# Hybrid decoder trunk on one core: SwiGLUs 2 to 4 with one plain block and five pairs, reciprocal-root factors, and block 0's second weight parts by accumulating DMA

## The chip, the cores and the metric

The kernel runs on one core of a Trainium2 chip. The metric is the device time of one execution in microseconds (us). The kernel before takes 1728.46 us, the median of 3 runs (1728.2 to 1728.85).

## What is computed

Two layers over 512 tokens of width 1024, all in float32. Each layer is

```python
x = x + 0.5 * swiglu(rms_norm(x, ffn1_norm[l]), ffn1_wg[l], ffn1_wu[l], ffn1_wd[l])
h = rms_norm(x, mix_norm[l])
z = h @ w_in[l]            # attention heads and a gated short convolution
x = x + concat([attn_out, conv_out]) @ w_out[l]
x = x + 0.5 * swiglu(rms_norm(x, ffn2_norm[l]), ffn2_wg[l], ffn2_wu[l], ffn2_wd[l])
```

with `swiglu(h, wg, wu, wd) = (silu(h @ wg) * (h @ wu)) @ wd`, 2816 columns in `wg` and `wu`, and a last `rms_norm`. So there are four SwiGLUs: number 1 opens layer 0, number 2 ends it, numbers 3 and 4 do the same in layer 1.

## The kernel before

**Three matmuls for one.** Every float32 operand is split into a rounded first part (`hi`) and the remainder (`lo`), and a product is `hi*hi + hi*lo + lo*hi`. `split` (L185) makes the two parts of a weight unit: ScalarE (ACT in the profile) casts `hi` (L186), VectorE (DVE) subtracts to get `lo` (L187). A weight unit is 512 KB in SBUF, 128 partitions by 1024 numbers. `need_split` (L189) makes the parts of unit n+2 when the group of unit n is taken (`SPLIT_AHEAD = 2`). The parts rotate through three buffers each (`wh`, `wl`), so the parts of unit n+3 can be made once the matmuls of unit n are through. Raw weights come from HBM through SyncE's queue into eight buffers tagged `raw`, four units ahead or more (`need_raw`, L173). Where a form needs the sum of two weights, GpSimd (POOL) issues a second, accumulating DMA into the same raw buffer (L181).

**Blocks.** The 2816 columns are 11 blocks of 256. A *plain* block (`plain`, L587) is 4 groups of 24 matmuls of 512 columns (`group`, L233): two gate groups and two up groups. Its gate is `silu(acc * inv) * inv`, because the groups run on the unnormalised `x * gain` while the norm's factors `inv` are still being made. A *Winograd* block (`winograd`, L608) works on the normalised input: seven half products (`CHAINS`, L46) of 24 matmuls of 256 columns. A *pair* (`winograd2`, L682) does two blocks at once with seven half products of 24 matmuls of 512 columns; each of its seven steps takes two weight units, h = 0 and 1. A pair's result lies token by token, so it is turned afterwards by 16 transposes in 4 turns (`turn`, L740), which wait in a list `pending` and are issued one by one by `flush`.

**Forms.** The seven half products need seven forms of the normalised input, `b11, b21, t2, t3, t1, t4, b22` in this order. `scale` (L407) makes the normalised input `full` (tile `hf`) with 8 DVE instructions, and `make` (L424) builds a form from it: sums on DVE where the form has them, then a split.

**Order of a SwiGLU.** `STAGES` writes it out: plain blocks 0 and 1, the down projection of block 0 (`("d", (0,))`, 8 groups of 6 matmuls), pair 2, down of block 1, pair 4, down of 2 and 3, pair 6, down of 4 and 5, pair 8, down of 6 and 7, Winograd block 10, down of 8, 9, 10. The forms are made during plain block 1 and the down projection of block 0, with `t4` and `b22` right after it. Inside this order the framework's scheduler places the instructions of each engine when the kernel is built: on an engine, the first in program order that it expects to be ready goes next.

**Norm.** While the stage before ends, `take` (L354) and `square` (L365) prepare each chunk of `x` as it is finished. `factors` (L391) sums the squares over partitions with two matmuls (tile `ssq`), placed inside the second group at its step 5. Then come ACT's square root (tile `root`, L404), ACT's mean (L405), and on DVE a reciprocal (L342) and one Newton step (L343 to L345), which give `inv`.

**End.** In the last SwiGLU `Finale` transposes `x` during block 10 and computes the down projection of blocks 8, 9, 10 token by token, in two halves of 512 columns, with the last norm's root after each group of tokens (`root`, L843).

Of the kernel before, what the change touches and what calls it, by code (L numbers as in the profile page):

```python
# [51 lines left out]
def trunk_kernel(  # L52
# [136 lines left out]
    def need_split(g):  # L189
        while state["split"] <= min(g, len(order) - 1):  # L190
            n = state["split"]
            u, what = order[n]
            if what is None or what == "wide":
# [78 lines left out]
    def plan():  # L272
        def cols(src, k0, kc, n):
            wide = abreast(kc)
            for b in range(0, n, wide):
                order.append((add_unit((src, k0, kc, b * P, wide * P)), None))

        def up(wg, wu, b):
            if b < PLAIN:
                for w in (wg, wu):  # L280
                    for j in range(2):
                        order.append((add_unit((w, 0, KC, (2 * b + j) * P, P)), None))
                return
# [21 lines left out]
        def ffn(wg, wu, wd, last=False):  # L305
            for what, b in STAGES:
# [6 lines left out]
                if not last or b[-1] < FF // (2 * P) - 1:  # L313
                    cols(wd, 2 * b[0], 2 * len(b), KC)
                    continue
# [6 lines left out]
        for l in range(DEPTH):  # L322
            ffn(ffn1_wg[l], ffn1_wu[l], ffn1_wd[l])
# [4 lines left out]
            ffn(ffn2_wg[l], ffn2_wu[l], ffn2_wd[l], l == DEPTH - 1)  # L328
# [11 lines left out]
    def newton(out, root, mean, spare):  # L340

        nc.vector.reciprocal(spare, root)  # L342
        nc.vector.tensor_mul(out, spare, spare)  # L343
        nc.vector.scalar_tensor_tensor(mean, mean, -0.5, out, op0=ALU.mult, op1=ALU.mult)
        nc.vector.scalar_tensor_tensor(out, mean, 1.5, spare, op0=ALU.add, op1=ALU.mult)  # L345

    class Norm:
# [32 lines left out]
        def groups(self, n, accs=()):  # L380
# [3 lines left out]
            while len(accs) < n:  # L384
                at, step = (1, 5) if self.i else (3, 2)
# [6 lines left out]
        def factors(self, parts):  # L392
# [11 lines left out]
            nc.scalar.activation(r, sp, AF.Sqrt, scale=1.0 / D, bias=eps)  # L404
            nc.scalar.activation(v, sp, AF.Identity, scale=1.0 / D, bias=eps)  # L405
            newton(self.inv, r, v, r)

        def scale(self):
# [12 lines left out]
            self.sums = [stock(f"sum{n}_{self.i}", shape=(P, KC // 2, H)) for n in range(2)]  # L421
# [107 lines left out]
    with tc.manual_schedule(engines={pe, act, dve}):  # L529
# [4 lines left out]
        first = group(norm.h, arrive)  # L534
# [6 lines left out]
    def first_parts():  # L541
# [3 lines left out]
        nc.scalar.activation(r, v, AF.Sqrt, scale=1.0 / D, bias=eps)  # L545
        nc.vector.tensor_scalar(v, v, 1.0 / D, EPS, op0=ALU.mult, op1=ALU.add)
        newton(y, r, v, r)
# [35 lines left out]
    def ffn(norm, after=None, late=None):  # L583

        acts = {}

        def plain(b):  # L587
# [16 lines left out]
            if norm.inv is None:  # L604
                accs = norm.groups(4, [first] if norm.i == 0 else [])
# [18 lines left out]
        def winograd(b, between=None):  # L624
# [18 lines left out]
            for step, (acc, operand, start) in enumerate(CHAINS):  # L643
# [34 lines left out]
                if between:  # L678
                    between(step)
            acts[b] = (hi, lo)  # L680

        def winograd2(b):  # L682
# [3 lines left out]
            accs = {  # L686
                c: [psum(tag, [P, S], f"{c}_{name}_{u}") for u in range(2)]
                for c, tag in (("x", "mm"), ("y", "sc"), ("w", "aux"))
            }
# [8 lines left out]
            for step, (acc, operand, start) in enumerate(CHAINS):  # L698
                xh, xl = norm.forms[operand]
                for h in range(2):  # L700
# [36 lines left out]
                    flush()  # L737
# [16 lines left out]
        def flush():  # L754
            if pending:
                pending.pop(0)()

        end = None
        for i, (what, b) in enumerate(STAGES):
            if what == "w":  # L760
                winograd2(b)
            if what == "u" and b < PLAIN:
# [3 lines left out]
            elif what == "u":  # L766
                if after is None:
                    end = Finale()
                winograd(b, end and end.step)
            if what != "d":  # L770
                continue
            rhs = [(acts[k][0][:, j, :], acts[k][1][:, j, :]) for k in b for j in range(2)]
            final = i + 1 == len(STAGES)
            if final and end:
                end.down(rhs)
# [10 lines left out]
            if b == (0,):  # L786
# [4 lines left out]
    class Finale:  # L791
# [3 lines left out]
        def __init__(self):  # L795
            self.y = [
                g4(f"ytok{t}", F32, (P, D)) if t < 2 else stock(f"ytok{t}", shape=(P, D))
                for t in range(NT)
            ]
# [3 lines left out]
        def step(self, n):  # L803

            for at in (0, 1) if n == 0 else (n + 1,):
                t, half = divmod(at, 2)
                tp = psum("mm", [P, S], f"yt_{t}_{half}")
# [8 lines left out]
        def widen(self, half, pairs):  # L816
            for i in range(pairs):
                if half == 0:
                    _, hi, lo = take_split()
                else:  # L820
                    u = len(units) - pairs + i
                    need_raw(u)
                    hi, lo = (form(f"ww{n}_{i}", shape=(P, 2, S)) for n in "hl")
                    split(hi, lo, raw_of.pop(u))
                self.w[half].extend((hi[:, k, :], lo[:, k, :]) for k in range(2))

        def piece(self, rhs, half, t, c0, wide, ssq):

            tok = slice(t * P, (t + 1) * P)
            acc = psum("mm", [P, wide], f"end_{half}_{t}_{c0}")  # L830
            cols = slice(c0, c0 + wide)
            for k, (ah, al) in enumerate(rhs):
# [3 lines left out]
                nc.tensor.matmul(acc, al[:, tok], wh[:, cols], start=False, stop=k == len(rhs) - 1)  # L836
# [4 lines left out]
            if half == 0:  # L841
                nc.gpsimd.tensor_mul(y, y, self.gain[half][:, cols])

        def root(self, t, ssq, rest):

            r, v, y = (small(f"{n}_end{t}", 1) for n in "rvy")
            nc.scalar.activation(r, ssq, AF.Sqrt, scale=1.0 / D, bias=rest)
            nc.vector.scalar_tensor_tensor(v, ssq, 1.0 / D, rest, op0=ALU.mult, op1=ALU.add)
            nc.vector.reciprocal(y, r)
            nc.vector.tensor_mul(r, y, y)  # L850
            nc.vector.scalar_tensor_tensor(r, r, -0.5, v, op0=ALU.mult, op1=ALU.mult)
            nc.vector.scalar_tensor_tensor(y, r, 1.5, y, op0=ALU.add, op1=ALU.mult)
            return y

        def down(self, rhs):
# [7 lines left out]
            self.widen(0, len(rhs) // 2)  # L863
            for t in range(NT):
                rest = done[:, t : t + 1]
                self.piece(rhs, 0, t, 0, S, rest)
                nc.vector.tensor_scalar(rest, rest, 1.0 / D, EPS, op0=ALU.mult, op1=ALU.add)
                if t == 0:
                    self.widen(1, len(rhs) // 2)
            for t in range(NT):  # L870
# [4 lines left out]
                for i in range(steps):  # L875
                    ssq = small(f"ssq_end{t}_{i}", 1)
                    self.piece(rhs, 1, t, i * wide, wide, ssq)
# [210 lines left out]
    for l in range(DEPTH):  # L1088
        n1, n2, n3 = Norm(3 * l + 1), Norm(3 * l + 2), Norm(3 * l + 3)
        ffn(norm, into(n1), make_bias if l == 0 else None)  # L1090
        mix(l, n1, into(n2))
        ffn(n2, into(n3) if l + 1 < DEPTH else None)
# [31 lines left out]
```

## Time and profile before

| what | value |
|---|---|
| median of 3 runs | 1728.46 us |
| the profiled execution's own time | 1728.36 us |
| its span (first to last instruction) | 1726.6 us |
| TensorE (PE) busy | 1717.1 us, 8156 matmuls |
| DVE busy | 1245.8 us |
| ACT busy | 825.3 us |
| POOL busy | 141.6 us |
| granted TensorE clock | 1.00 |
| HBM read | 224.96 MB |

A matmul's length in the profile (389 ns for 512 columns) is from its start to its end in the pipeline; the next one starts 227 ns after it. So PE's busy share does not tell how densely matmuls follow one another. The starts in the timeline do.

### The profile page before, as it was taken

The page shows a single profiled execution, that of the slowest core. Times are in us where ns is not written, and L with a number is a line of the kernel's source. Part 1 is how long each engine was busy: PE and PEld are TensorE (multiplying, and loading weights), DVE is VectorE, ACT ScalarE, POOL GpSimd, SP SyncE. Part 2 cuts the span into 40 slices and gives each one's busy share as a digit, 9 for nine tenths or more (in the row PEclk, how much of TensorE's full clock was granted, in tenths as well). Part 3 has the DMA queues.
Part 4 walks back from the last instruction along what each step waited for, and adds up shares of the span by engine and source line. Part 5 has one row for each costly group of instructions (what it writes and reads, how often), then busy time and mean ns, then how long its engine had stood idle before and what let it go on. Part 6 is the DMA issues. An engine that isn't in the chain of part 4 may idle for free.

```text
span 1726.6 us, 21261 instructions
## 1 busy us (share of the span) xinstructions
PE 1717.1 (99%) x8156; PEld 1433.1 (83%) x8156; DVE 1245.8 (72%) x1722; ACT 825.3 (48%) x1219; POOL 141.6 (8%) x127
## 2 busy tenths in 40 slices
PE   9999999999999999999999999999999999999998
PEld 7888888988888888888888888888888888888897
DVE  7986666678758876666688776666787598776664
ACT  6544443556544543543545434434565445444443
POOL 1011000001200011000000010000022001011001
PEclk9999999999999999999999999999999999999999
DMA  8467455422334566644445666444124347557431
GB/s 245 111 163 205 131 136 149 132 73 62 110 98 98 152 165 159 181 124 119 138 99 158 159 157 183 125 120 140 55 62 124 97 98 187 154 134 195 132 113 49
DMA packets 217241, 228.44 MB, mean 132 GB/s; under 512 B 7404, under 2 KB 152372, under 8 KB 217140
## 3 DMA queue, kind: packets, MB, share of 16 engines
q1 hardware_dynamic: 194356, 187.89, 35.9%
q0 software_dynamic: 21632, 37.75, 13.4%
q8 instruction: 64, 1.05, 0.2%
q10 hardware_dynamic: 1152, 1.45, 0.2%
q14 instruction: 37, 0.30, 0.1%
HBM read 224.96 MB, written 2.10 MB: 132 GB/s over the span
## 4 chain that ended last, share of the span: by engine, by line
PE 96%; DVE 2%; ACT 1%; DMA 0%; issue 0%; SPq 0%; ACTq 0%
PE x L708 20%; PE acc L246 17%; PE acc L249 17%; PE acc L253 16%; PE y L708 10%; PE w L708 5%; PE x L652 3%; PE at L744 2%; PE y L652 1%; PE w L652 1%; PE end L836 1%; PE end L834 1%; PE end L835 1%; PE pt L995 1%; DVE p L988 0%; ACT p L980 0%
## 5 line engine op out<-in xcount | busy, mean ns | idle before, releaser
L186 ACT CAST wh<-raw 128x1024 fp32r<-128x1024 f32 (+2 forms) x429 | 444.6, 1037 | 646.4 <-PE acc L249 287.1
L187 DVE TENSOR_TENSOR wl<-raw,wh 128x1024 fp32r<-128x1024 f32 (+2 forms) x428 | 520.2, 1217 | 233.4 <-ACT wh L186 231.5
L246 PE MATMUL acc<-ah,wh 128*128 128x512 f32 x656 | 261.6, 399 | 0.0
L253 PE MATMUL acc<-ah,wl 128*128 128x512 f32 x656 | 256.5, 391 | 0.0
L249 PE MATMUL acc<-al,wh 128*128 128x512 f32 x656 | 255.4, 389 | 0.0
L246 PE MATMUL acc<-xh,wh 128*128 128x512 f32 x544 | 213.8, 393 | 0.1
L249 PE MATMUL acc<-xl,wh 128*128 128x512 f32 x544 | 212.5, 391 | 0.1
L780 DVE SCALAR_TENSOR_TENSOR x<-acc,x 128x512 f32<-128x512 f32 x184 | 124.7, 688 | 109.8 <-PE acc L253 109.1
L253 PE MATMUL acc<-xh,wl 128*128 128x512 f32 x512 | 199.8, 390 | 0.0
L253 PEld LDWEIGHTS acc<-ah,wl 128*128 128x128 f32 x656 | 123.3, 188 | 26.5
L249 PEld LDWEIGHTS acc<-al,wh 128*128 128x128 f32 x656 | 123.5, 188 | 23.7
L246 PEld LDWEIGHTS acc<-ah,wh 128*128 128x128 f32 x656 | 123.3, 188 | 23.3
L249 PEld LDWEIGHTS acc<-xl,wh 128*128 128x128 f32 x544 | 102.2, 188 | 21.9 <-DVE xl L363 1.6
L246 PEld LDWEIGHTS acc<-xh,wh 128*128 128x128 f32 x544 | 102.2, 188 | 21.0 <-issue 0.5
L181 POOL DMA_DIRECT2D raw<-in_ffn_wu_dram x36 | 43.8, 1220 | 852.0 <-DVE u L732 377.8
L253 PEld LDWEIGHTS acc<-xh,wl 128*128 128x128 f32 x512 | 96.1, 188 | 20.1
L181 POOL DMA_DIRECT2D raw<-in_ffn_wg_dram x36 | 43.8, 1216 | 288.7 <-DMA raw<-in_ffn_wu_dram 171.0
L186 ACT CAST ah<-at 128x512 fp32r<-128x512 f32 x64 | 37.4, 585 | 62.5 <-PE at L744 62.2
L187 DVE TENSOR_TENSOR al<-at,ah 128x512 fp32r<-128x512 f32 x64 | 43.6, 687 | 9.2 <-ACT ah L186 8.7
L708 PE MATMUL x<-wh,fb11h 128*128 128x512 f32 x128 | 49.8, 389 | 0.0
L708 PE MATMUL x<-wh,fb11l 128*128 128x512 f32 x128 | 49.8, 389 | 0.0
L708 PE MATMUL x<-wl,fb11h 128*128 128x512 f32 x128 | 49.8, 389 | 0.0
(297 smaller groups left out, 3338.9 us busy)
## 6 DMA issues: line engine op xcount, KB each, us to landing
raw<-in_ffn_wu_dram SPq DMA_DIRECT2D x124, 512.0 KB, 3.7
raw<-in_ffn_wg_dram SPq DMA_DIRECT2D x87, 512.0 KB, 3.9
raw<-in_ffn_wd_dram SPq DMA_DIRECT2D x70, 512.0 KB, 3.6
raw<-in_ffn_wu_dram POOLq DMA_DIRECT2D x36, 512.0 KB, 7.1
raw<-in_ffn_wg_dram POOLq DMA_DIRECT2D x36, 512.0 KB, 6.1
raw<-in_w_in_dram SPq DMA_DIRECT2D x36, 512.0 KB, 3.7
raw<-in_ffn_wd_dram SPq DMA_DIRECT2D x24, 384.0 KB, 3.4
raw<-in_w_out_dram SPq DMA_DIRECT2D x16, 512.0 KB, 3.7
```

What stands on the lines that cost most here:

```text
L181: nc.gpsimd.dma_start(out=r, in_=rows_of(*more), accum_op=ALU.add)
L186: nc.scalar.copy(hi, raw)
L187: eng.tensor_sub(lo, raw, f32(hi))
L246: nc.tensor.matmul(acc, hi[:, k, :], rhs[k][0], start=k == 0, stop=False)
L249: nc.tensor.matmul(acc, hi[:, k, :], rhs[k][1], start=False, stop=n == 0 and k == last)
L253: nc.tensor.matmul(acc, lo[:, k, :], rhs[k][0], start=False, stop=k == last)
L652: nc.tensor.matmul(out, w[:, k, cols], x_[:, k, :], start=start and k + i == 0, stop=k == KC // 2 - 1 and i == 2, skip_group_check=not start,)
L708: nc.tensor.matmul(out, x_[:, 2 * h + k, tok], w[:, k, :], start=start and h + k + i == 0, stop=h + k == 2 and i == 2, skip_group_check=no ...
L744: nc.tensor.transpose(tp[:, t * P : (t + 1) * P], ups[t][:, c * P : (c + 1) * P], ident)
L780: nc.vector.scalar_tensor_tensor(xs[c], acc, 0.5, xs[c], op0=ALU.mult, op1=ALU.add)
L834: nc.tensor.matmul(acc, ah[:, tok], wh[:, cols], start=k == 0, stop=False)
L835: nc.tensor.matmul(acc, ah[:, tok], wl[:, cols], start=False, stop=False)
```

## The change

- **Order.** SwiGLU 1 keeps its order (`FIRST`). SwiGLUs 2, 3 and 4 get one plain block and five pairs: plain block 0, down of block 0, pairs 1 and 3, down of 1 and 2, pair 5, down of 3 and 4, pair 7, down of 5 and 6, pair 9, down of 7 and 8, down of 9 and 10. In SwiGLU 4 the last two are one, done by `Finale`, which begins with blocks 7 and 8.
- **Forms.** In SwiGLUs 2 to 4 `b11` is made inside plain block 0, between its two up products; `b21`, `t2`, `t3` during the down projection of block 0; `t1`, `t4`, `b22` during the first three steps of pair 1. The two buffers for sums move from the tag `raw` to the tag `g4`.
- **Turns.** `flush` is called once after each of a pair's steps 0 and 1 and twice after step 2 (before: after each half step).
- **Factors.** ACT's function is `Abs_reciprocal_sqrt`, so DVE's reciprocal goes; `ssq` stands at step 2 of the second group (before: 5) in every norm but the first.
- **Second parts.** For the six weight units of plain block 0 and its down projection in SwiGLUs 2 to 4 (`"far"`), ACT writes minus the first part to `lo` and the first part to `hi`, and GpSimd issues an accumulating DMA that adds the raw weight to `lo`, SBUF to SBUF.

```diff
-STAGES = (
-    ("u", 0), ("u", 1), ("d", (0,)), ("w", 2), ("d", (1,)), ("w", 4), ("d", (2, 3)), ("w", 6),
+FIRST = (
+    ("p", 0), ("p", 1), ("d", (0,)), ("w", 2), ("d", (1,)), ("w", 4), ("d", (2, 3)), ("w", 6),
     ("d", (4, 5)), ("w", 8), ("d", (6, 7)), ("u", 10), ("d", (8, 9, 10)),
 )
-PLAIN = 2
+INNER = (
+    ("p", 0), ("d", (0,)), ("w", 1), ("w", 3), ("d", (1, 2)), ("w", 5), ("d", (3, 4)), ("w", 7),
+    ("d", (5, 6)), ("w", 9), ("d", (7, 8)), ("d", (9, 10)),
+)
+LAST = INNER[:-2] + (("d", (7, 8, 9, 10)),)
...
-            if n:
+            if what == "far":
+                nc.scalar.activation(lo, raw, AF.Copy, scale=-1.0)
+                nc.scalar.copy(hi, raw)
+                nc.gpsimd.dma_start(out=f32(lo), in_=raw, accum_op=ALU.add)
+            elif n:
                 split(hi, lo, raw)
...
-    def newton(out, root, mean, spare):
-        nc.vector.reciprocal(spare, root)
-        nc.vector.tensor_mul(out, spare, spare)
+    def newton(out, guess, mean):
+        nc.vector.tensor_mul(out, guess, guess)
...
-                at, step = (1, 5) if self.i else (3, 2)
+                at, step = (1, 2) if self.i else (3, 2)
...
-            nc.scalar.activation(r, sp, AF.Sqrt, scale=1.0 / D, bias=eps)
+            nc.scalar.activation(r, sp, AF.Abs_reciprocal_sqrt, scale=1.0 / D, bias=eps)
...
-                norm.scale()
+                norm.scale(stock if first else g4)
                 up(0, accs[2])
+                if not first:
+                    norm.make("b11")
                 up(1, accs[3])
...
-                    flush()
+                if step < 3:
+                    flush(2 if step == 2 else 1)
+                if between:
+                    between(step)
+                if not first and step < 3:
+                    ahead = CHAINS[step + 4][1]
+                    if ahead not in norm.forms:
+                        norm.make(ahead)
...
-                if b == (0,) and c in (0, 4):
-                    norm.make("t3" if c == 0 else "t1")
+                if b == (0,):
+                    made = {0: "t3", 4: "t1"} if first else {0: "b21", 2: "t2", 5: "t3"}
+                    if c in made:
+                        norm.make(made[c])
...
+            ready = blocks[:-2]
+            take(ready)
+            for i in range(len(ready)):
+                self.widen(0, i, pairs)
+            accs = [psum("mm", [P, S], f"end_0_{t}") for t in range(NT)]
+            for t in range(NT):
+                self.products(accs[t], rhs, 0, t, 0, 0, len(rhs))
+                flush()
+            take(blocks[-2:])
```

More of the change, by code (lines that the diff above doesn't have):

```diff
@@ L192, in need_split @@
             u, what = order[n]
[L193 removed]
+            if what in (None, "wide", "far"):
                 need_raw(u + LOAD_AHEAD)
@@ L303, in up2, with ffn @@
             order.extend((u, (what, h)) for what in FORMS for h in range(2))
-        def ffn(wg, wu, wd, last=False):
-            for what, b in STAGES:
+        def ffn(wg, wu, wd, stages):
+            for what, b in stages:
+                how = "far" if b in (0, (0,)) and stages is not FIRST else None
+                if what == "p":
+                    plain(wg, wu, b, how)
                 if what == "u":
@@ L533, in trunk_kernel @@
         turn_x(0)
-        first = group(norm.h, arrive)
+        opening = group(norm.h, arrive)
         squares(0)
@@ L580, in make_bias, with ffn @@
             )
-    def ffn(norm, after=None, late=None):
+    def ffn(norm, stages, after=None, late=None):
         acts = {}
+        first = stages is FIRST
         def plain(b):
@@ L677, in winograd, with winograd2 @@
                         split(hi[:, m, :], lo[:, m, :], up)
-                if between:
-                    between(step)
             acts[b] = (hi, lo)
-        def winograd2(b):
+        def winograd2(b, between=None):
             name = f"{norm.i}_{b}"
[L686 to L689, printed above, removed]
+            accs = {}
             gates = [g2(f"gate_{name}_{t}") for t in range(NT)]
@@ L698, in winograd2 @@
             for step, (acc, operand, start) in enumerate(CHAINS):
+                if operand not in norm.forms:
+                    norm.make(operand)
                 xh, xl = norm.forms[operand]
+                if start:
+                    tag = {"x": "mm", "y": "sc", "w": "aux"}[acc]
+                    accs[acc] = [psum(tag, [P, S], f"{acc}_{name}_{u}") for u in range(2)]
                 for h in range(2):
@@ L752, in ffn, with flush @@
         pending = []
-        def flush():
-            if pending:
-                pending.pop(0)()
+        def flush(n=1):
+            for _ in range(n):
+                if pending:
+                    pending.pop(0)()
         end = None
-        for i, (what, b) in enumerate(STAGES):
+        for i, (what, b) in enumerate(stages):
             if what == "w":
-                winograd2(b)
-            if what == "u" and b < PLAIN:
+                if after is None and b == 9:
+                    end = Finale()
+                winograd2(b, end and end.step)
+            if what == "p":
                 plain(b)
@@ L795, in __init__ @@
         def __init__(self):
[L796 to L799, printed above, removed]
+            self.y = []
             self.w = [[], []]
@@ L814, in step, with widen, products @@
                 nc.scalar.copy(self.y[t][:, half * S : (half + 1) * S], tp)
[L816 to L827, printed above, removed]
+        def widen(self, half, i, pairs):
+            if half == 0:
+                _, hi, lo = take_split()
+            else:
+                u = len(units) - pairs + i
+                need_raw(u)
+                hi, lo = (form(f"ww{n}_{i}", shape=(P, 2, S)) for n in "hl")
+                split(hi, lo, raw_of.pop(u))
+            self.w[half].extend((hi[:, k, :], lo[:, k, :]) for k in range(2))
+        def products(self, acc, rhs, half, t, c0, a, b):
             tok = slice(t * P, (t + 1) * P)
-            acc = psum("mm", [P, wide], f"end_{half}_{t}_{c0}")
-            cols = slice(c0, c0 + wide)
-            for k, (ah, al) in enumerate(rhs):
+            cols = slice(c0, c0 + acc.shape[1])
+            for k in range(a, b):
+                ah, al = rhs[k]
                 wh, wl = self.w[half][k]
```

95 lines of the change are left out of this document (54 added, 41 removed).

## The prediction

> **What bounds the kernel now.** I read the page first, then PE's waits, the chain of waits in order of time, the timelines of PE, DVE and ACT around the start of SwiGLU 2 (520 to 613 us), and the busy time by stretch.
>
> ```profile
> span 1726.6 us, 21261 instructions
> PE 96%; DVE 2%; ACT 1%; DMA 0%; issue 0%; SPq 0%; ACTq 0%
> ```
>
> The chain is PE for 96% of the span. PE's own waits are three:
>
> ```profile
> PE idle L113 <- DVE warm L472: 1.2, 1, 1.2
> PE xt L490 <- DMA xin<-in_x_dram: 0.8, 1, 0.8
> PE o L1010 <- DVE pl L999: 0.7, 2, 0.4
> ```
>
> None lies in SwiGLUs 2 to 4. So there a microsecond of matmuls saved is a microsecond of the end, if nothing new makes PE wait. The chain in order of time gives the price of matmuls, a pair's step (L708) and a Winograd block's (L652), 24 matmuls each:
>
> ```profile
> 575.16 5.44 PE x L708 x24
> 580.61 5.44 PE w L708 x24
> ...
> 811.42 2.87 PE x L652 x24
> 814.29 2.88 PE w L652 x24
> ```
>
> 5.44 / 24 = 0.2267 us for 512 columns, 2.877 / 24 = 0.1199 us for 256 columns, more than half of the former.
>
> DVE is the second limit. Busy time by stretch (PE, PEld, DVE, ACT, POOL) from the factors' end to pair 2's start, and from there to the second parts for its fourth step:
>
> ```profile
> 536.80:574.98 38.18, 38.18 (x170) 31.63 (x169) 36.63 (x55) 18.61 (x26) 3.61 (x3) 1.00 0.41 94
> 574.98:591.30 16.32, 16.32 (x73) 13.52 (x72) 16.32 (x20) 9.82 (x13) 1.19 (x1) 1.00 0.60 135
> ```
>
> DVE is busy 36.63 of 38.18 us and then 16.32 of 16.32, and PE just does not wait. The change shortens this stretch; that is where it is decided.
>
> **What PE saves.** Each of SwiGLUs 2 to 4 loses a plain block, 96 x 0.2267 = 21.76 us, and a Winograd block, 168 x 0.1199 = 20.14 us. It gets a pair, 168 x 0.2267 = 38.09 us, and its four turns:
>
> ```profile
> 110.23 0.38 PE L744 MATMUL at<-ident,u 128*128 128x128 f32 x2
> ...
> 112.06 0.38 PE L744 MATMUL at<-ident,u 128*128 128x128 f32 x2
> ```
>
> Between these starts lie one turn and six matmuls, so a turn is 1.83 - 6 x 0.2267 = 0.47 us, four are 1.88. Saved: 41.90 - 39.97 = 1.93 us a SwiGLU, 5.8 in three. The down projections keep their number of matmuls.
>
> **What goes from DVE, and when the factors come.** Origin T is block 0's first matmul (520.12 before). Now `ssq` is at T+8.84, and
>
> ```profile
> 530.34 3.35 DVE L342 RECIPROCAL root<-root 128x512 f32<-128x512 f32 x1 [2.50 <-ACT root L404]
> ```
>
> then a weight split and three short instructions give `inv` at T+16.7. After: `ssq` stands after 24 + 6 matmuls, at T+6.80, and ends at 7.03 + 0.39 = 7.42. Its input, `sql`, ended at T+4.9; ACT's extra copy ahead of `xh` delays that by at most 1.0, so it fits. ACT first makes both copies of a far unit, released at T+5.41: 2 x 0.96, to 7.35. Table load 1.28 and root 0.69: 9.3 (as many table loads as before, so only their place counts; I price the new function as the old). Newton by the spacing of the old rows, 0.72 + 0.72 + 0.69: `inv` at T+11.45.
>
> **What PE then needs, and what DVE must do by then.** Block 0 ends at 0.45 + 21.76 = 22.2, its down projection (48 x 0.2267 = 10.88) at 33.1, and pair 1's first three steps at 49.4. The third matmul of step 4 needs a second part; four matmuls that do not need it can be ahead: T+50.3.
>
> DVE's list from `inv` to that second part, in program order, by spacings of the DVE timeline (two in 1.28 and one in 0.68: 0.60 for 512 numbers; 0.665 for `hf`; 0.61 for `x` at L780; 1.135 for 1024 numbers): 28 of 0.60 (8 for gates and up products, 16 for `b11`, `b21`, `t2`, `t3`, `t1` and sums, 2 sums of `t4`, 2 gates of pair 1) = 16.8; 8 `hf` = 5.3; 8 `x` = 4.9; 7 splits and 4 sums of weights (L203, L224) = 12.5. Sum 39.5, so T+51.0 and 0.1 to land: 51.1, **0.8 us late**. The same count on the kernel before gives 52.5 us, against 54.3 measured from 536.8 to 591.1, 1.2 of them a first wait, so the list is good to about a microsecond. Without the far DMAs there would be two more splits in it.
>
> Just before, the down projection of block 0 needs block 0's last up product, whose group ends only at T+22.2 and then takes DVE 0.60, ACT 0.6, DVE 0.68 and whatever DVE has in hand: about T+24.5 to 25.9. Before, a whole plain block lay between. PE has three matmuls a group on the first up product and, with four PSUM buffers, 12 such matmuls (2.7 us) to T+24.9, if the scheduler moves them ahead. It does such things:
>
> ```profile
> 106.64 0.27 PE L744 MATMUL at<-ident,p 128*128 128x128 f32 x1
> 106.67 0.48 PE L246 MATMUL acc<-ah,wh 128*128 128x512 f32 x1
> ...
> 108.00 0.33 PE L744 MATMUL at<-ident,p 128*128 128x128 f32 x1
> ```
>
> A fourth transpose that was not ready gave way to five matmuls of the next group. So this costs 0 to 1.0 moved, about 2.9 in order (25.9 against 22.9); a wait here also gives DVE time, so the two do not add. Per SwiGLU I take 0.6 us of new waiting: between 0 (a late split served first) and the ledger's 0.8, nearer the ledger. Three: 1.8 us.
>
> **The far DMAs.** Ahead of ACT's copies stand its casts; queued behind each far DMA on POOL are the pairs' accumulating DMAs. SBUF to SBUF is not in the trace; the nearest rows are the HBM accumulates:
>
> ```profile
> 538.86 1.20 POOL L181 DMA_DIRECT2D raw<-in_ffn_wu_dram  x1 [59.93 <-DMA raw<-in_ffn_wu_dram]
> ...
> DMA to landing us min/median/max: 5.7/6.4/10.7
> ```
>
> From a buffer's release to need there are two groups and two matmuls, 10.88 + 0.45 us; ACT's copies take 2.0, so a landing up to 9.3 us hides. I take 6.4 to 8, cost nothing. Lower bound 3.7 (a plain load), upper 10.7. The Trainium skill, "DMA: Bandwidth & Descriptors", section on the anatomy of one DMA on the GpSimd path, has about 2.0 us plus bytes over 436 GB/s, which for 512 KB would be an estimate of 3.2 us. By that this risk would vanish and the sum stay; the rows here, 5.7 at least, speak against it.
>
> **The rest.** ACT gets 18 copies of 0.96 us; it is busy 18.61 of 38.18 us, so they hide, apart from the place counted above. Pair after pair (1 and 3) asks 20 loads and 8 accumulates in 78 us. By the queues' shares each load takes the 16 engines 1.7 us and each accumulate 3.2, together 60 of 78 us: hidden, without cover 0 to 1 us. `d(9, 10)` gives DVE 4.9 of every 5.44 us while the next norm is prepared: hidden, else up to 0.5. The earlier factors of the two mixes meet the only PE waits there (0.7 in all): 0 to 0.7 gained, taken as 0. `Finale` makes its fourth split in a buffer freed 2.7 us before need, and the split takes 2.4: 0 to 0.5, taken as 0. Its last root loses DVE's 0.16 us reciprocal and the gap around it: 0.2 gained at the very end. SwiGLU 1, the flushes, the moved sum buffers: nothing.
>
> **Sum.** 1728.36 - 5.8 + 1.8 - 0.2 = 1724.2 in the profiled execution's own time, which lies 0.1 under the median: **1724.3 us**.
>
> **The rivals.**
> - *PE keeps its order at block 0's down projection.* 3 x 2.9 in place of 1.8: 1728.46 - 6.0 + 8.7 = 1731.2. For it: a plan made at build time moves matmuls only where it expects the wait, and the mixes' waits (0.7 us, above) show that it misses some. Against: the transposes above.
> - *Far DMAs land late: slower.* It decides from 9.3 us. At the trace's 10.7 the excess of 1.4 us comes once for every two units, three times a SwiGLU: 4.2, three SwiGLUs 12.6, less what it hides of the DVE list (2.4): 1728.46 - 6.0 + 10.2 = 1732.7. For it: pair 1's own accumulates are issued on the same queue in these 20 us. Against: the median of 6.4.
> - *DVE is held during POOL's issue.* Two issues of 1.20 us in the DVE list: 2.4 more each, 1724.3 + 7.2 = 1731.5. The Trainium skill's "SBUF — State Buffer", who interferes with whom, has a DVE instruction with two SBUF inputs blocked by a GpSimd instruction that reads SBUF. The trace does not bear that out for issues: five `hf` beside the issue at 544.28 took 3.40 us (0.664 apart), three without one 2.07 (0.663).
> - *Nothing new waits*, and the mixes gain: 1728.46 - 6.0 - 0.7 = 1721.8. Against: the DVE list, dense before already.
>
> **Chances.** Forecast 0.58, spread by the waiting of 0 to 1.5 us a SwiGLU over 1722.5 to 1727; order kept 0.17; late DMAs 0.12; DVE held 0.03; nothing waits 0.10. A measurement tells about 0.2%, 3.5 us, from no change. Faster (under 1725.0): 0.42 of the forecast and the last, 0.52. Same: 0.16 and nearly all of order kept and DVE held, 0.35. Slower: 0.13. The range runs from 1721.7 to 1731.5; it leaves out the late DMAs and the edges of the others, under 2 in 10.
>
> **What would show it.** The pairs' matmuls should be 19 x 168 = 3192 (now 2688), the Winograd block's 168 (now 672), the turns' transposes 304 (now 256), with no reciprocal of 128x512. Right if PE's waits name second parts (`wl`) or a form in pair 1 for under 1 us; wrong if they name `al`, `ah` at the first down projection for 2 us or more, or the far `wl` DMA. Wrong as well if DVE's list takes over 41 us from `inv`.

## The result, and the profile after

The changed kernel takes **1738.42 us** (median of six runs, 1734.70 to 1741.42), the kernel before 1728.50 (1728.20 to 1728.85) beside it: the ratio is 1.0055 with an interval of 1.0042 to 1.0068. It is slower by 9.9 us, where 4.2 us less were forecast. The profiled execution took 1734.70, the shortest of the six, so what its trace shows is the smaller part of the loss: its span is 6.1 us longer than that of before. The span and the chain's shares, from the page of after:

```profile
span 1732.7 us, 20824 instructions
...
PE 84%; issue 6%; DVE 5%; DMA 4%; ACT 1%; POOL 0%; SPq 0%; POOLq 0%; ACTq 0%; DVEq 0%
```

The chain was PE for 96%; now it leaves PE for DMA, DVE and "issue". PE's own waits in after (total us, times, longest):

```profile
PE acc L262 <- DMA wl<-raw: 5.4, 3, 2.5
...
PE y L722 <- DVE wl L191: 0.5, 3, 0.2
```

Both are new. The first is the far DMA of a second part, once in each of SwiGLUs 2 to 4; the second is the split for pair 1's fourth step.

A table by stage shows more than the waits, since PE also loses time when its order was made for another arrival. Each stage is its length from PE's timeline, less its matmuls at 0.2267 us:

| stage, us over its matmuls in SwiGLUs 2, 3, 4 | after | no wait would be |
|---|---|---|
| block 0 | 3.32, 2.11, 2.58 | 0.48 (the two `ssq` products) |
| its down projection | 0.21, 0.19, 0.19 | 0 |
| pairs 1 and 3, one behind the other | 3.48, 3.47, 3.47 | 1.90 (four turns) |
| all later stages | as before | as before |

From start to start, SwiGLU 2 takes 346.48 us (343.96 before), SwiGLU 3 345.25 (343.94), SwiGLU 4 to the end of the span 356.4 (354.4). SwiGLU 1 and the two mixes take what they took. So 6.6 us are lost in block 0 and 4.7 in the pairs, 11.3 in all, against the 5.4 that SwiGLUs 2 to 4 save in the last experiment, where neither of the two is left: that is the 6 us of the profiled run.

The busy time by stretch (PE, PEld, DVE, ACT, POOL), from the factors to pair 1's start, and over its first three steps:

```profile
533.00:556.64 23.64, 21.17 (x92) 16.81 (x91) 20.93 (x33) 12.68 (x18) 4.10 (x4) 1.00 0.98 216
556.64:575.00 18.36, 18.11 (x79) 14.34 (x79) 18.36 (x23) 11.23 (x16) 0.00 (x0) 1.00 0.23 63
```

DVE is as full as forecast in the second (18.36 of 18.36 us). But in the first it has 2.7 us to spare, and there PE loses most: 21.17 of 23.64. The share of the DMA engines, second from the right, is 0.98 there. That is where to look.

### The profile page after: what moved, and what is told of

It reads as the page before. It is cut to its first block, busy times and chain, and to the rows that moved or that the text cites. A ratio compares the mean times of both kernels' runs of the same rounds, so it can differ in the third digit from the quotient of the medians.

```text
span 1732.7 us, 20824 instructions
## 1 busy us (share of the span) xinstructions
PE 1717.6 (99%) x7922; PEld 1416.9 (82%) x7922; DVE 1217.9 (70%) x1685; ACT 850.8 (49%) x1236; POOL 164.4 (9%) x151
## 4 chain that ended last, share of the span: by engine, by line
PE 84%; issue 6%; DVE 5%; DMA 4%; ACT 1%; POOL 0%; SPq 0%; POOLq 0%; ACTq 0%; DVEq 0%
PE x L722 22%; PE acc L255 12%; PE acc L258 12%; PE acc L262 12%; PE y L722 12%; PE w L722 5%; DMA wl<-raw 3%; PE at L766 2%; DVE wl L191 2%; DMA raw<-in_ffn_wu_dram 1%; PE end L857 1%; PE end L859 1%; PE end L858 1%; PE x L666 1%; PE pt L1043 1%
## 5 line engine op out<-in xcount | busy, mean ns | idle before, releaser
L190 ACT CAST wh<-raw 128x1024 fp32r<-128x1024 f32 (+2 forms) x415 | 432.8, 1045 | 617.9 <-PE acc L258 219.3
L191 DVE TENSOR_TENSOR wl<-raw,wh 128x1024 fp32r<-128x1024 f32 (+2 forms) x414 | 507.3, 1227 | 231.6 <-ACT wh L190 230.4
L255 PE MATMUL acc<-ah,wh 128*128 128x512 f32 x640 | 254.1, 399 | 0.0
L255 PE MATMUL acc<-xh,wh 128*128 128x512 f32 x448 | 176.5, 394 | 0.1
L258 PE MATMUL acc<-xl,wh 128*128 128x512 f32 x448 | 175.2, 391 | 0.1
L262 PE MATMUL acc<-xh,wl 128*128 128x512 f32 x416 | 163.0, 392 | 5.4 <-DMA wl<-raw 5.4
L255 PEld LDWEIGHTS acc<-ah,wh 128*128 128x128 f32 x640 | 120.0, 188 | 23.6 <-ACT ah L190 1.0
L185 POOL DMA_DIRECT2D raw<-in_ffn_wu_dram x39 | 47.1, 1211 | 671.5 <-DVE u L746 343.6
L258 PEld LDWEIGHTS acc<-xl,wh 128*128 128x128 f32 x448 | 84.2, 188 | 18.3 <-DVE xl L374 1.6
L255 PEld LDWEIGHTS acc<-xh,wh 128*128 128x128 f32 x448 | 84.2, 188 | 17.3 <-issue 0.5
L262 PEld LDWEIGHTS acc<-xh,wl 128*128 128x128 f32 x416 | 78.1, 188 | 23.4 <-DMA wl<-raw 7.1
L190 ACT CAST ah<-at 128x512 fp32r<-128x512 f32 x76 | 44.1, 584 | 67.6 <-PE at L766 67.6
L185 POOL DMA_DIRECT2D raw<-in_ffn_wg_dram x39 | 46.9, 1204 | 234.5 <-DMA raw<-in_ffn_wu_dram 153.4
L722 PE MATMUL x<-wh,ft1h 128*128 128x512 f32 x152 | 59.7, 392 | 0.2
L722 PE MATMUL y<-wh,ft3h 128*128 128x512 f32 x152 | 59.6, 392 | 0.3
L722 PE MATMUL x<-wh,ft2h 128*128 128x512 f32 x152 | 59.5, 392 | 0.0
```

The source lines that it names most:

```text
L185: nc.gpsimd.dma_start(out=r, in_=rows_of(*more), accum_op=ALU.add)
L190: nc.scalar.copy(hi, raw)
L191: eng.tensor_sub(lo, raw, f32(hi))
L255: nc.tensor.matmul(acc, hi[:, k, :], rhs[k][0], start=k == 0, stop=False)
L258: nc.tensor.matmul(acc, hi[:, k, :], rhs[k][1], start=False, stop=n == 0 and k == last)
L262: nc.tensor.matmul(acc, lo[:, k, :], rhs[k][0], start=False, stop=k == last)
```

## Where the far DMAs stood

ACT's timeline of after, in block 0 of SwiGLU 2 (start, us, engine and line): the negated copy of the fourth unit, and the new root.

```profile
526.83 1.05 ACT L226 ACTIVATE wl<-raw 128x1024 fp32r<-128x1024 f32 x1
...
529.20 0.69 ACT L415 ACTIVATE root<-ssq,eps 128x512 f32<-128x512 f32 x1
```

The copy is done at 527.88, and PE could use the finished second part from about 538.0 on (540.43 less its wait of 2.47, in the row of PE below): 10.1 us for the DMA. POOL's timeline of the same stretch, with what ended the idle time before each issue in brackets:

```profile
520.56 1.20 POOL L185 DMA_DIRECT2D raw<-in_ffn_wu_dram  x1 [2.39 <-DMA raw<-in_ffn_wu_dram]
522.75 0.89 POOL L228 DMA_DIRECT2D wl<-raw  x1 [0.99 <-ACT wl L226]
530.27 1.20 POOL L185 DMA_DIRECT2D raw<-in_ffn_wu_dram  x1 [6.63 <-DMA raw<-in_ffn_wu_dram]
530.99 1.40 POOL L228 DMA_DIRECT2D wl<-raw  x1
```

The far DMA (L228) is issued at 530.99, 3.1 us after its copy was done. In front of it in POOL's order stands an accumulating DMA of pair 1 (L185), whose result DVE reads at 563.56 at the earliest, 33 us later, and the bracket says what that one waited for: its own plain load. Issued 0.7 us apart, the two then run together, and the far DMA takes 9.4 us to land. On PE:

```profile
540.43 0.50 PE L262 MATMUL acc<-xh,wl 128*128 128x512 f32 x1 [2.47 <-DMA wl<-raw]
```

And the plain load was late because of the far DMAs: on SP's own queue 18 plain loads wait for a `raw` buffer until a far DMA has read it, 113.5 us in all, up to 9.5 each. For the place shown, the trace has it link by link: the second unit's far DMA, issued at 517.30, lands at 522.54; the plain load into the buffer that it frees goes out at 522.59 and lands at 529.68; the accumulating DMA on that buffer is the one at 530.27. It is a ring: far DMA, buffer, plain load, accumulating DMA, next far DMA.

The theories to be told apart:
- **Q**, the queue: the accumulating DMA ahead in POOL's order, waiting for its load, makes the far DMA late.
- **L**, the landing: SBUF to SBUF is too slow by itself, in whatever order.
- **D**, DVE: the list from the factors to pair 1 decides, and the DMA's wait only fills time that DVE would take anyway.

## The experiments

The kernel before was run beside each of these kernels; its median was 1728.5 to 1728.6 each time. A diff is against the changed kernel if nothing else is said.

### No far DMA at all

```diff
-                how = "far" if b in (0, (0,)) and stages is not FIRST else None
+                how = None
```

> The changed kernel with the ordinary split for all six units of block 0 and its down projection; nothing else differs. Theory Q (queue): the far second parts come late because GpSimd's queue and ring put pair 1's accumulating DMAs ahead of them; those waits cost 6.6 us in the profiled execution (1734.7) and about 10.3 at the median of 1738.4. They vanish here, and the runs lie within 1 us of each other again. DVE's list from the factors to pair 1's fourth step gets two more splits (2.3 us), so pair 1's waits grow from 1.6 to at most 3.9 us a SwiGLU: 1728.1 to 1735.0. Rival L (landing): SBUF to SBUF accumulation is slow and uneven by itself; the same numbers here. Rival D (DVE): the waits for DMA hide a DVE list that would be late anyway; then without them pair 1's waits grow by as much as the DMA waits go, and the time stays at 1736 or more.

Measured: 1734.9 us (1734.0 to 1736.4), ratio 1.0039 [1.0027, 1.0052]. Better than the change, but 6.4 above before. The wait for `wl` is gone, and another stands in its place, at the start of block 0's down projection: `PE acc L255 <- ACT ah L190`, 4.4 us in three; with the matmuls that then come out of their order, block 0 and its down projection take about 2 us more a SwiGLU than in the next kernel. DVE's timeline shows why: the two splits for that projection stand ahead of block 0's first up product (L613), which is the input of `ah`.

```profile
540.35 1.22 DVE L191 TENSOR_TENSOR wl<-raw,wh 128x1024 fp32r<-128x1024 f32 x1
...
543.47 0.68 DVE L613 TENSOR_TENSOR gate<-acc,gate 128x512 f32<-128x512 f32 x1
```

From block 0's first matmul the up product starts at 21.4 us here, at 19.2 in the next kernel, which has two splits of 1.14 us fewer ahead of it. So theory D holds for this kernel: far DMAs are of use, but which of them?

### Far DMAs for the down projection's two units alone

```diff
-                how = "far" if b in (0, (0,)) and stages is not FIRST else None
+                how = "far" if b == (0,) and stages is not FIRST else None
```

> Only the two units of block 0's down projection are far; the four of plain block 0 are split on DVE, which has 4 us without work before the factors come. Theory Q: the late one is the fourth unit, behind an accumulating DMA; without it the block's waits go from 6.6 (10.3 at the median) to 1 or less, and pair 1's 4.7 in all stay: 1728 to 1729. Rival L: the two far units left still land 9 us after issue at times and wait, about half the cost stays: 1733. Rival D: 1736 or more, in pair 1.

Measured: 1728.28 us (1727.8 to 1728.95), ratio 1.0000 [0.9991, 1.0009]. Block 0 takes 22.24 us, its matmuls and the `ssq` products, with no wait; the far DMAs land in 4.4 to 5.6 us. Two of six far units bring back all 10 us. The four that go were for block 0 itself; there no far DMA holds a `raw` buffer now, and POOL issues pair 1's two accumulating DMAs at 516.71 and 524.33 (520.56 and 530.27 in the changed kernel), ahead of both far DMAs.

### Six far units, pair 1 without its accumulating DMAs

```diff
+            if b == 1:
+                parts = tuple(what[:1] for what in parts)
```

Pair 1's sums of weights lack their second term here, so it computes with other weights; the number of splits, sums and matmuls stays.

> The changed kernel, all six units far, but pair 1 of SwiGLUs 2 to 4 loads only the first weight of each sum: its four accumulating DMAs are left out, so the pair computes with other weights. Instructions on PE, DVE and ACT are the same. Theory Q: nothing stands before the far DMAs on GpSimd's queue or in their ring, they land 4.4 to 5.5 us after issue each time, PE never waits for them: about 1728, narrow. Rival L: landings of 7 to 9 us stay, and PE's waits of 5 us or more with them: 1736 to 1738. Rival D: as L in time, but the waits move to pair 1.

Measured: 1728.37 us (1727.8 to 1728.8), ratio 1.0000 [0.9992, 1.0009]. Nothing waits for `wl<-raw`; the far DMAs land in 4.4 us at least, 5.5 in the median, 7.1 at most. **Theory L falls**: the landing alone, at most 7.1 us, stays under the limit. But this kernel also leaves out transfers, so it does not tell the queue's order from the sharing of bandwidth.

### The same six far units, the accumulating DMAs behind them

```diff
-                nc.gpsimd.dma_start(out=r, in_=rows_of(*more), accum_op=ALU.add)
+                held.append((r, more))
...
-                nc.gpsimd.dma_start(out=f32(lo), in_=raw, accum_op=ALU.add)
+                ins = nc.gpsimd.dma_start(out=f32(lo), in_=raw, accum_op=ALU.add)
+                if order[n + 1][1] != "far":
+                    with tc.issue_after(ins.ins):
+                        release()
```

`release` issues what `held` holds; `issue_after` binds only the order on the queue. No work is left out or added.

> The changed kernel with its six far units a SwiGLU, in which only the order on POOL's queue is another: the two accumulating DMAs of pair 1 that stood between the far DMAs are issued behind the last of them. Same work, same bytes. Theory Q (a far DMA is late because POOL's queue is taken in order and an accumulating DMA that still waits for its plain load stands ahead of it): the waits of PE for wl<-raw go (6.6 us of block 0 over the three SwiGLUs, less what they covered), each block 0 takes 22.2 us, the run comes to 1728.3 (1727.5 to 1729.5), like the kernels with two far units and without the accumulating DMAs. If the two transfers merely share the bandwidth of the rings, and the order on the queue means nothing: 1732 or more, with the wait for wl<-raw at 1 us or more a SwiGLU. Rival D (DVE alone decides) has the run stay at 1734 to 1738.

Measured: 1728.44 us (1727.97 to 1728.66), ratio 0.9999 [0.9990, 1.0008]. POOL's timeline of this kernel in the same stretch:

```profile
522.75 0.85 POOL L237 DMA_DIRECT2D wl<-raw  x1 [4.57 <-ACT wl L235]
528.19 0.85 POOL L237 DMA_DIRECT2D wl<-raw  x1 [4.59 <-ACT wl L235]
```

The fourth unit's far DMA goes out at 528.19 in place of 530.99, each is issued as soon as ACT has made the copy, and they land in 4.4, 5.7 and 7.1 us (minimum, median, maximum) in place of 4.4, 7.4 and 9.5. The order on one queue is the whole 10 us between the two medians, and the spread too: 0.7 us over these runs against 6.7. **Theory Q is shown**: the order in which POOL issues the transfers makes the loss.

The order does two things at once, and no experiment here parts them. In both profiles of the changed kernel every wait of PE for `wl<-raw` is for the fourth unit's far DMA. That DMA goes out 2.1 to 4.2 us after its copy is done, behind the accumulating DMA, and then takes 7.7 to 10.1 us to land, with that transfer under way. By estimate either half alone would cost little against the 10.1 us there are: the longest delay, 4.2, with the median landing of 5.7 makes 9.9, and an issue 0.3 us after the copy, as here, with the longest landing makes 10.4. It is the sum that is too long.

### The changed kernel once more

Its runs spread, and the one profiled was the shortest; a second profile asks where a longer one is longer.

> The changed kernel once more, for a second profile: its runs spread from 1734.7 to 1741.4, and the profiled one was the shortest. Theory Q: what a longer run has more is in the waits of block 0 for wl<-raw (5.4 us in the first profile, block 0 6.6 us over its matmuls), SwiGLU by SwiGLU, and the pairs take 79.6 as before. If the spread is somewhere else (the clock, the pairs, the mixes), those stretches differ and block 0 does not.

Measured: 1739.97 us, one run, span 1738.1, 5.4 us over the first profile. Block 0 is 7.51, 1.30 and 2.74 us over its matmuls, 3.5 us more than in the first profile; 1.65 us lie ahead of SwiGLU 2, in the kernel's start, and 0.2 in no one place. The pairs take what they took.

The 3.5 us are not all waiting. PE's waits for `wl<-raw` come to 6.3 us here, 0.9 more than in the first profile. In SwiGLU 2 the longest of them, 3.83 us, is followed by slow matmuls. First PE's timeline, then the busy time of a stretch, with the granted clock third from the right:

```profile
543.36 0.79 PE L262 MATMUL acc<-xh,wl 128*128 128x512 f32 x1 [3.83 <-DMA wl<-raw]
543.96 0.63 PE L255 MATMUL acc<-xh,wh 128*128 128x512 f32 x1
...
549.50 0.44 PE L258 MATMUL acc<-xl,wh 128*128 128x512 f32 x1
549.78 0.39 PE L262 MATMUL acc<-xh,wl 128*128 128x512 f32 x1
```

```profile
544.00:548.00 4.00, 4.00 (x11) 3.13 (x10) 0.69 (x2) 0.00 (x0) 0.00 (x0) 0.50 1.03 254
```

The granted clock is 0.50, and from 543.96 to 549.50 thirteen matmuls take 5.54 us in place of 13 x 0.2267 = 2.95: 2.6 us that are not in any list of waits. In the first profile, where the longest wait was 2.47 us, the clock stays at 1.00 in block 0. So the expectation's other answer, the clock, holds for the larger part of the 3.5 us, though only right behind the longest wait for a far DMA. The mean granted clock points the same way for the runs without a trace: 0.999 in the shortest of the six runs of the changed kernel, 0.997 or 0.998 in the other five, 0.997 here; that the same stretch stands in them is likely, but not shown.

### The reciprocal-root table alone, in the order before

This is the kernel before, with the table's root in place of root and reciprocal, and `ssq` after step 2 of the group.

```diff
-            nc.scalar.activation(r, sp, AF.Sqrt, scale=1.0 / D, bias=eps)
+            nc.scalar.activation(r, sp, AF.Abs_reciprocal_sqrt, scale=1.0 / D, bias=eps)
...
-            newton(self.inv, r, v, r)
+            newton(self.inv, r, v)
```

> The kernel before with the second part of the change alone: the reciprocal-root function, no DVE reciprocal, the sums of squares at step 2 of the second group. All theories: PE waits for none of this before, so only the 0.2 us at the very end can show: 1728.3. If the earlier sums of squares make PE wait, 1729 or more.

Measured: 1728.31 us (1728.0 to 1729.0), ratio 1.0001 [0.9992, 1.0009]: nothing. With two plain blocks DVE has time for its reciprocal.

### The pairs: forms one step later

With the far DMAs mended the change stands at 1728.3 to 1728.4, like before: the other half of the loss, 1.57 us a SwiGLU in the pairs, still eats what the matmuls save. The kernel with two far units shows two places. In pair 1 of SwiGLU 3, DVE:

```profile
913.87 1.28 DVE L454 TENSOR_TENSOR sum<-sum,hf 128x512 f32<-128x512 f32 x2
915.07 1.21 DVE L191 TENSOR_TENSOR wl<-raw,wh 128x1024 fp32r<-128x1024 f32 x1
```

and PE:

```profile
916.34 0.50 PE L722 MATMUL y<-wl,ft3h 128*128 128x512 f32 x1 [0.17 <-DVE wl L191]
```

The split for step 4 lands at 916.3, and PE waits for it. Just ahead of it DVE makes the sums for `t4`, which only step 6 uses. The experiment, on the kernel with two far units:

```diff
-                    ahead = CHAINS[step + 4][1]
+                    ahead = CHAINS[step + 3][1]
```

> The kernel with far DMAs for the two down projection units alone (1728.28), and in pair 1 each of the forms t1, t4 and b22 is made one step later, so that the weight splits of steps 3 and 4 stand ahead of them in DVE's order. Theory F (pair 1's loss of some 0.8 us is DVE's list: forms stand ahead of the splits that are due sooner): pair 1 runs at its own matmuls (38.1 us), the two pairs take 78.8 in place of 79.6, three times 0.8 is won: 1725.9 (1725.2 to 1726.8). If the list is too long as a whole, the wait only moves to the steps that use the forms, and the run stays at 1728.3.

Measured: 1725.85 us (1725.5 to 1727.2), ratio 0.9985 [0.9976, 0.9994]. The two pairs take 78.77, 78.80 and 78.78 us in place of 79.6. The wait for `wl` in pair 1 is gone, none appears at the forms.

### The pairs: turns two and two

The second place is ahead of pair 3's fourth step, PE in SwiGLU 3 of the kernel with two far units:

```profile
954.82 0.38 PE L766 MATMUL at<-ident,p 128*128 128x128 f32 x2
955.03 0.38 PE L766 MATMUL at<-ident,u 128*128 128x128 f32 x2
955.25 0.38 PE L766 MATMUL at<-ident,p 128*128 128x128 f32 x2
955.71 0.50 PE L722 MATMUL x<-wh,ft1h 128*128 128x512 f32 x1
```

Behind the two turns should come `y<-wh,ft3h`, step 4. But `y` sums in the two PSUM buffers (`sc`) that the turns have just filled and that ACT and DVE must first read. So PE goes on with step 5 (`ft1h`), whose second parts are not there yet; 0.71 us is lost in four gaps. (PE's list of waits does not name them; that the two buffers are the reason is read from the program, and the experiment is to bear it out.) The experiment, again on the kernel with two far units, keeps every turn a whole step (5.4 us) or more away from step 4:

```diff
-                if step < 3:
-                    flush(2 if step == 2 else 1)
+                if step < 2:
+                    flush(2)
```

> The kernel with far DMAs for the two down projection units alone (1728.28), and where pair 3 follows pair 1 its four turns come two behind step 1 and two behind step 2, none behind step 3. Theory T (the two turns just ahead of step 4 hold the two PSUM buffers that step 4 is to sum in, so PE takes step 5's matmuls first, ahead of their weights; 0.7 us a SwiGLU is lost there): the pairs take 78.9 in place of 79.6, 1726.2 (1725.5 to 1727.3). If the two turns behind step 1 come too early, because pair 1's last up products are not ready then, PE waits there for p instead, and the run is 1728.3 or more.

Measured: 1725.99 us (1725.75 to 1726.34), ratio 0.9986 [0.9977, 0.9995]; the pairs take 78.80, 78.90 and 78.95 us.

### Both

> Far DMAs for the two down projection units alone, forms one step later, turns two and two. Theory F and T together: the two losses lie 30 us apart and add, 3 x (0.8 + 0.7) = 4.5: 1723.8 (1723.0 to 1725.0), within 0.5 of the predicted time of the changed kernel, and faster than both kernels. If one of the two only fills slack that the other leaves, 1726 or more.

Measured: 1723.36 us (1723.20 to 1723.57), ratio 0.9970 [0.9958, 0.9982]. The two gains add (2.4 and 2.3 apart, 4.9 together), the pairs take 77.97 to 78.10 us: their matmuls and four turns, with no wait. It beats both kernels.

### The same, with root and reciprocal as before

```diff
-            nc.scalar.activation(r, sp, AF.Abs_reciprocal_sqrt, scale=1.0 / D, bias=eps)
+            nc.scalar.activation(r, sp, AF.Sqrt, scale=1.0 / D, bias=eps)
             nc.scalar.activation(v, sp, AF.Identity, scale=1.0 / D, bias=eps)
+            nc.vector.reciprocal(r, r)
```

> The fastest kernel so far (two far units, forms later, turns two and two; 1723.36), with the inner norms' root and DVE's reciprocal of 3.35 us as before the change; the place of the sum of squares stays. In the order before the change the table was worth nothing (1728.31 against 1728.51). Theory R (with one plain block DVE's list from the factors to pair 1 bounds PE, and 3.35 us more on it show): PE waits for ah at the first down projection and for wl in pair 1, 2 to 3.3 us in each of three SwiGLUs: 1729.4 to 1733.3. If DVE has that much slack in this order: 1723.4 to 1724.5.

Measured: 1733.98 us (1732.65 to 1735.63), ratio 1.0032 [1.0021, 1.0043]: 10.6 us more than with the table, just above the edge given. The profiled run (1734.07) loses all of it around the start of block 0's down projection, where PE waits:

```profile
PE acc L255 <- ACT ah L190: 6.0, 3, 2.0
```

The waits, 6.0 us, are not all of the loss. In each of SwiGLUs 3 and 4 block 0 and its projection take 3.1 us longer than with the table, close to the reciprocal's 3.35, since the matmuls around the wait also come out of their order. SwiGLU 2 takes another 1.5 us: from 546 to 549 us the granted clock is 0.50 there, and after the same wait it stays up in the other two. In the order before, the table, with the earlier `ssq` besides, was worth nothing. Of the expected two places only `ah` shows; pair 1 does not wait, because PE's wait for `ah` has given DVE its time back.

### The change with its three losses mended

Six far units with the accumulating DMAs behind them, forms one step later, turns two and two.

> All six far units with the accumulating DMAs of pair 1 behind them, forms one step later, turns two and two: the change as it was meant, with its three losses mended. Theory Q with F and T: like the kernel with two far units, 1723.4, perhaps 0.3 less because SwiGLU 2's first down projection loses 0.2 in place of 0.5: 1722.8 to 1723.6. If four splits fewer on DVE still gain something, 1722.5 or less; if far DMAs cost somewhere else, 1724 or more.

Measured: 1723.33 us (1722.61 to 1723.54), ratio 0.9969 [0.9958, 0.9981]. The chain of this kernel is PE's again:

```profile
PE 96%; DVE 2%; ACT 1%; DMA 0%; issue 0%; SPq 0%; ACTq 0%; DVEq 0%
```

SwiGLU 2 takes 342.07 us and SwiGLU 3 342.10, 1.9 and 1.8 less than before: what the prediction's step on the matmuls gives (1.93). The four far units of plain block 0 win nothing over the two of its projection alone (1723.36): the four splits that they spare DVE stand ahead of the factors, where DVE is idle for 4.09 us in the changed kernel.

## Why the prediction was wrong

**The step that failed** is "The far DMAs", in its words "I take 6.4 to 8, cost nothing". The limit of 9.3 us was well worked out (10.1 measured, from ACT's copy to the need), and the landing itself fits: 4.4 to 7.1 us where nothing stands in the way. What the step left out is the time before the landing. It had the queue the wrong way round, "queued behind each far DMA on POOL are the pairs' accumulating DMAs"; two of them stand ahead, and while one waits for its plain load, every far DMA behind it waits as well: 3.1 us in the place shown, and 9.4 to land beside it. That an accumulating DMA waits so could be read from the row of POOL that the prediction shows, at 538.86: its bracket ends in `<-DMA raw<-in_ffn_wu_dram`. The rival "Far DMAs land late: slower" was priced from a landing alone, 10.7 at most, and given 0.12; its mechanism with the queue in it is what happened, at 6.6 us in one profile and 10.1 in the other (2.6 of these are matmuls at half the clock, which no sum had), against its 12.6 less 2.4. That its price comes near is luck: it had the landing three times a SwiGLU, and only one in each is waited for. The sign that the prediction had named for being wrong, a wait of PE for the far `wl`, is the one that came.

The sentence on the accumulating DMAs' queue was the place to work this out: a DMA issue is an instruction, it waits in its queue, and it holds up what stands behind it (6.63 us in POOL's row at 530.27). The Trainium skill, "DMA: Bandwidth & Descriptors", section on the anatomy of one DMA on the GpSimd path, has the first half of this rule: the DMA engines wait for no semaphore, the issuing engine does so before it hands the transfer on; the trace agrees, with those 6.63 us. The second half, that a transfer behind it waits along, is what the order experiment shows. The estimate of 3.2 us by the same section, which the prediction weighed, is too low for these accumulating DMAs: no far DMA landed in under 4.4. To see the wait before the run, one had to ask for each issue on POOL not only how long it lasts but what it waits for; the answer (a plain load, which waits for a buffer, which a far DMA holds) is in the program.

**What PE saves**: right. 1.93 us a SwiGLU was worked out; 1.9, 1.8 and 1.7 are seen in the last experiment, with 0.2 lost at the first down projection in each.

**When the factors come**: right. T+11.45 forecast, 11.7 in SwiGLU 2 of after (ends at 532.14, T at 520.47). The root's row above has the 0.69 us that was taken from the old function.

**What DVE must do**: right in mechanism and size. The split for step 4 was put at T+51.1; in the kernel with two far units it lands at 916.3 with T at 865.02, T+51.3. The lateness of 0.8 us a SwiGLU is what making the forms later wins back (0.8 each); PE's list of waits names 0.2 of it, the rest are gaps between matmuls taken out of their order. The 0.6 us taken was a little low. The step counts a list in program order, and here that order was exactly what cost.

**The down projection of block 0**: right. The scheduler moves matmuls ahead; 0.2 us is lost, within 0 to 1.0. "Order kept" did not come.

**The rest**: one term was missed. "Pair after pair (1 and 3)" was priced for its loads and accumulating DMAs (hidden, as forecast), and the four turns inside pair 3 at 0.47 us each, but not for the PSUM buffers that turns and step 4 share: 0.7 us a SwiGLU, the same size as DVE's lateness. SwiGLU 1 and the mixes: nothing, as forecast. DVE held during POOL's issue: not seen; four `hf` beside the far DMA's issue at 534.14 take 2.73 us in after, 0.68 apart, and so do the four from 537.31 on.

In sum, for the profiled run: -5.4 (matmuls and end, the 0.6 of the three first down projections taken off; -6.0 forecast), +4.7 in the pairs (+1.8 forecast for all new waiting there and at the down projections), +6.6 for the far DMAs (0 forecast): about 6 slower. Without the far DMAs' loss the kernel stands at 1728.4, not faster either: the forecast was 4.1 us too low even there, 2.9 of it in the pairs. The median of the changed kernel lies 3.7 us above the profiled run.

What is not settled: block 0 loses 0.8 us in one SwiGLU and 7.0 in another of the same run. Of the 7.0, about 4.0 are the wait and 3.0 the slow matmuls behind it. Why the wait itself is 0.5 us in one place and 3.8 in another is open: the ring of buffer, load and accumulating DMA leaves room for it, but no run here changed one link of it at a time. Nor is it settled after which wait the clock falls: it fell after 3.83 us, not after 2.47 in the other profile, and in the kernel with the reciprocal after one wait of 2.0 us and not after two others as long.

## What to carry to other kernels

An instruction that issues a DMA waits in its engine's queue like any other: before a new transfer is put on a queue, list what stands ahead of it there and what each of those waits for, and put transfers that are due later behind it by an explicit order. A gain that vanishes may hide several losses: mended one at a time, the change first came level with the kernel before (1728.4) and then, with two small edits worth 2.4 and 2.3 us, to 1723.3. A wait of PE can also cost more than its length, so the matmuls behind it have to be read too. A part that is worth nothing in one order (the reciprocal-root table, 0.2 us) can be worth 10.6 us in another, where it has become the bound.

## What the runs showed of the hardware

An accumulating DMA from SBUF to SBUF of 512 KB lands 4.4 us after its issue at best, 5.7 in the median with six in a row, and up to 10.1 beside accumulating DMAs from HBM. After a wait of PE of 3.83 us the granted clock was 0.50 for some 6 us, and a matmul of 512 columns took 0.43 us from start to start in place of 0.227. Abs_reciprocal_sqrt over 128x512 takes ACT 0.69 us, like the root, and its table load 1.28 us; with the same three correction instructions behind it, it saves the whole 3.35 us reciprocal.
